# Neighbourhood attention: the low parts of the keys in a tile of their own for each head, with zeros in the other head's rows

## The chip, the core and the metric

The kernel runs on one core of one Trainium2 chip. The metric is the device time in microseconds of one execution. The core has five engines with a queue each: TensorE (PE; its weight loads are recorded as PEld), VectorE (DVE), ScalarE (ACT), GpSimd (POOL) and SyncE (SP), which issues most of the DMAs.

## The reference

Two layers of a diffusion backbone, over 512 latent tokens and 256 context tokens of 1024 features. Layer 0 has neighbourhood attention (8 heads of 64) beside a bidirectional mLSTM (4 heads of 128), layer 1 a latent attention; each layer ends in a gated feed-forward network with a depthwise convolution. The change lies in the neighbourhood attention, of which this is the core:

```python
def row_block(args):                       # one row of the 64-wide grid
    ...
    s_lat = jnp.einsum('bqhd,bkhd->bhqk', q_row, k_band).astype(jnp.float32) * scale + bias
    s_ctx = jnp.einsum('bqhd,bkhd->bhqk', q_row, k_c).astype(jnp.float32) * scale
    p = jax.nn.softmax(jnp.concatenate([s_lat, s_ctx], axis=-1), axis=-1).astype(v.dtype)
    nl = kh * GRID_W
    return (jnp.einsum('bhqk,bkhd->bqhd', p[..., :nl], v_band)
            + jnp.einsum('bhqk,bkhd->bqhd', p[..., nl:], v_c))
```

A latent query sees its window of 8 rows by 16 columns and all context keys; context queries see the context keys. All is in float32.

## The kernel before

To keep float32 accuracy with faster products, each operand is split into a high part (rounded to the type fp32r) and a low part (the rest, rounded too), and the products high x high, high x low and low x high are added up in PSUM. A linear projection is thus three products for each tile of 128 input features (`proj_steps`, one step of three products at a time).

**The heads come in pairs.** Four pairs, `p_` = 0 to 3. `na_proj` projects queries, keys and values of a pair (PSUM tiles `qp`, `kp`, `vp`) and makes for each head `s` of the pair:

- `qs[s]`, 128 rows: the high part of the head's 64 query rows in its own rows (`r0:r1`), their low part in the other head's rows;
- `kd[s]`, 128 rows: the high part of the head's keys, twice, in both halves;
- `kl`, one tile for both heads: the low part of the keys, head 0 in rows 0 to 63, head 1 in rows 64 to 127.

One product of `qs[s]` with `kd[s]` over 128 rows so gives (q high + q low) x k high. A second product, over the head's 64 rows alone, adds q high x k low.

**Scores.** `na_attn` takes 4 blocks of 128 queries for each head. A block has four products of 256 columns into one PSUM tile `sp`: high and low with the latent window, high and low with the context. Then DVE adds the bias and takes the maximum (line 816), ACT takes the exponential, DVE the reciprocal of the sum and POOL scales (tile `P`). `weighted` transposes P (`ptp`), copies it out (`pT`) and multiplies it with the values (`ops`). `scores_c` and `weighted_c` do the same for the context's own queries (`spc`, `Pc`, `ptc`, `opc`): one set of four products for each head. The score tiles take turns in three PSUM banks (`ps_w`).

**What fills the waits.** While a pair is in attention, PE gets the projections of the next pair in between (`fill`, a number of steps behind each block); for the last pair it gets the first products of the output projection (`yps`). Pair 0's first blocks run while the mLSTM's last head ends: DVE normalises its output (`mix`, in `ml_out`), and PE transposes it (`hTp`). Pairs 0 and 2 keep their tiles in the pool `nqr`, pairs 1 and 3 in `nql`; each tile is used again two pairs later. The framework that builds the program sets the order on each engine; each engine runs its queue in order.

The weights of the depthwise convolution of both layers lie in one constant tile `fcw`, loaded by a DMA of POOL's at the start and used in `up_post` of the feed-forward networks.

Of the kernel before, what the change touches and what calls it, by code (L numbers as in the profile page):

```python
# [9 lines left out]
F32 = mybir.dt.float32  # L10
# [56 lines left out]
def hybrid_backbone_kernel(ctx: ExitStack, tc: tile.TileContext, *aps):  # L67
# [14 lines left out]
    def psum_open(**n):  # L82
        """n: tiles per tag; A tiles hold two banks, the others one"""
        if psum:
            psum["st"].close()
        st = ExitStack()
        psum["st"], psum["n"], psum["split"] = st, n, False
        psum["p"] = st.enter_context(tc.tile_pool(name="ps" + "".join(f"{k}{v}" for k, v in n.items()), bufs=1,
                                                  space=bass.MemoryType.PSUM, reuse_waits="tile"))
# [41 lines left out]
    fcw = cload("ffn_conv", [128, 2, 2 * NH, 4])  # L131
# [26 lines left out]
    def table(func, after):  # L158
        """has the activation table loaded ahead of its first use"""
        t = tiny.tile([128, 8], F32, tag="rv", name="tab")  # L160
        act(t[:, 0:1], after, func)

    def fr(ap):
        return ap.bitcast(F32)
# [18 lines left out]
    def proj(o, w, x, cols, ks=tuple(range(KD)), first=True, last=True):  # L183
        """out[m, cols] = sum over k tiles of W[k, m]^T x[k, cols]; w units hold [k][128]."""
        whi, wlo = w
        xhi, xlo = x
        for lo, hi, oo in cols:
            for k in ks:
                wh = whi[:, k * 128:(k + 1) * 128]
                wl = wlo[:, k * 128:(k + 1) * 128]  # L190
                oa = o[:, oo:oo + hi - lo]
                mm(oa, wh, xhi[:, k, lo:hi], first and k == ks[0], False)
                mm(oa, wh, xlo[:, k, lo:hi], False, False)
                mm(oa, wl, xhi[:, k, lo:hi], False, last and k == ks[-1])
# [50 lines left out]
    def ada(l, part, get, pool, bufs):  # L245
        """modulation part (1024 columns) of layer l; column group j of the array takes 256 of them"""
        acc = None
        for k in range(KD):
            yield
            acc = acc or get("ada")  # L250
            w = pool.tile([128, 4, 256], F32, tag="aw", name="aw", bufs=bufs)
            nc.sync.dma_start(out=w, in_=a["ada_w"][l, part, k].rearrange("p (a b) -> p a b", a=4))
            for j in range(4):
                PE.matmul(out=acc[32 * j:32 * j + 32, 0:256], lhsT=s32[:, k, :], rhs=w[:, j, :],
                          start=k == 0, stop=k == KD - 1, tile_position=(0, 32 * j))
        row = scratch("arow")
        act(row[:, 0:256], acc[:, 0:256])
        pt = get("adat")
        for b in range(2):
            mm(pt[:, 8 * b:8 * b + 8], row[:, b * 128:(b + 1) * 128], sel[:, 0:8], True, True)  # L260
        m = mod[l][:, part * 8:(part + 1) * 8, :].rearrange("p (j b) i -> p j b i", b=2)
        tt(V, m, pt[:, 0:16].rearrange("p (b j i) -> p j b i", b=2, i=2),
           adab[:, l, part * 8:(part + 1) * 8].rearrange("p (j b) -> p j b", b=2).unsqueeze(3)
           .to_broadcast([128, 4, 2, 2]), ALU.add)

    def ada_q(l, part, q, get, pool, bufs):
        """256 columns of a part; column group j of the array takes a quarter of the k tiles"""
# [16 lines left out]
    def ada_v(l, part, hf, nv, get, pool):  # L284
        """half a part of the modulation on the vector engine: the k tiles are scaled and added up, then the
        tensor engine sums over the partitions"""
# [40 lines left out]
    def mod_scale(l, part, norm, name, nv=2):  # L327
        """norm_g * (1 + scale)"""
        t = const.tile([128, KD, nv], F32, name=name)
        ts(V, t, mod[l][:, part * 8:(part + 1) * 8, 0:nv], 1.0, None, ALU.add, ALU.bypass)  # L330
        tt(V, t, t, ng[:, l, norm, :].unsqueeze(2).to_broadcast([128, KD, nv]), ALU.mult)
        return t
# [10 lines left out]
    class Seg:  # L343
        """a run of tokens: width, offset in the padded layout, offset in the packed one, modulation column"""
# [12 lines left out]
    def rstd_bc(pss, n, dim, name):  # L357
        """PSUM [128, n*128]: rstd of every token on all partitions"""
        return bcasts(rstd_of(pss[:, :n], n, dim), n, name)
# [15 lines left out]
    def step(n):  # L375
        """n steps of the norm chains in flight, oldest first"""
        while n and chains:
            try:
                next(chains[0][1])
                n -= 1  # L380
            except StopIteration:
                chains.pop(0)

    def until(sg):
        """finish the chain of a run of tokens"""
# [3 lines left out]
    def sums4(ps, w, srcs, first, last):  # L389
        """column sums of four tiles, side by side in the array"""  # L390
# [4 lines left out]
    def sums_bc(ps, sg, name):  # L395
        """rstd on all partitions from the sums of sums4"""
# [7 lines left out]
    class YNorm:  # L404
        """sum of squares over the feature tiles of a branch output, then the gated residual"""
# [27 lines left out]
        def chain(self, x, y, Gt, mod=None, done=None):  # L433
            """x(k) += y(k) * rstd * G, then h hi/lo = split(x(k) * rstd * A + B) with mod = (A, B, h), or done(k);
            a feature tile per step, y as scratch"""
# [38 lines left out]
    # =============================== layer 0 ===============================  # L474
# [4 lines left out]
    with ExitStack() as l0:  # L479
# [38 lines left out]
        def x0_scale(q):  # L518
            """x * rstd * A for a quarter of the feature tiles"""
# [16 lines left out]
        def token_major(which, wus):  # L536
            """W[k, 512] with tokens on the output partitions; a k tile per step"""
# [39 lines left out]
        # gate rows, four feature tiles side by side in the array; the shift comes in with the bias  # L577
# [58 lines left out]
        # tri[:, 0]: k <= m ; tri[:, 1]: k >= m ; tri[:, 2]: row 127 ; tri[:, 3]: row 0  # L636
# [12 lines left out]
        # additive masks: msk[:, 0] allows column <= row, msk[:, 1] allows column >= row  # L649
# [9 lines left out]
        # running maxima of e along the scan, chunks and heads on partitions (the directions 32 apart)  # L659
# [52 lines left out]
        # -M in three exact pieces (rows 0, 32, 64 on), for its sums over the partitions to be rows of it  # L712
# [30 lines left out]
        def na_proj(p_, nq, res):  # L743
            """queries, keys and values of a pair of heads, in steps"""
# [19 lines left out]
            kl = nq.tile([128, T], F32R, tag="kl", name="kl")  # L764
            for s in range(2):
                r0, r1 = (0, 64) if s == 0 else (64, 128)
                act(kd[s][r0:r1, :], kp_[r0:r1, 0:T])
                tt(V, kl[r0:r1, :], kp_[r0:r1, 0:T], fr(kd[s][r0:r1, :]), ALU.subtract)
# [22 lines left out]
        def na_attn(p_, nw, bias_t, fill, qs, kd, kl, vtok):  # L791
# [6 lines left out]
            def scores(s):  # L798
# [8 lines left out]
                for j in range(4):  # L807
                    sp = ps_w("sp")
                    q_ = qs[s][:, j * 128:(j + 1) * 128]
                    qh_ = qs[s][r0:r1, j * 128:(j + 1) * 128]  # L810
                    lat = sp[:, 0:256].rearrange("p (f r c) -> p f r c", f=2, r=8)
                    mm(lat, q_, klat(kd[s], j), True, False)
                    mm(lat, qh_, klat(kl[r0:r1], j), False, True)
                    mm(sp[:, 256:512], q_, kd[s][:, TX:T], True, False)
                    mm(sp[:, 256:512], qh_, kl[r0:r1, TX:T], False, True)
# [30 lines left out]
            def scores_c(s):  # L846
                r0, r1 = rows[s]
                sp = ps_w("spc")
                for j in range(2):
                    q_ = qs[s][:, TX + j * 128:TX + (j + 1) * 128]  # L850
                    qh_ = qs[s][r0:r1, TX + j * 128:TX + (j + 1) * 128]
                    mm(sp[:, j * 256:(j + 1) * 256], q_, kd[s][:, TX:T], True, False)
                    mm(sp[:, j * 256:(j + 1) * 256], qh_, kl[r0:r1, TX:T], False, True)
# [47 lines left out]
        if True:  # L901
# [4 lines left out]
            def ml_in(hd):  # L906
                qk = []
                for w_ in range(2):
# [9 lines left out]
                    # 2 silu(u) = (tanh(u / 2) + 1) u  # L918
# [16 lines left out]
            def ml_decay(hd, sT):  # L935
                """decay matrices times scores, both directions"""
                ws = []
                for d in range(2):
                    pump(MP[0][d])
                    # w^T[s, t]; fwd admits s <= t  # L940
# [108 lines left out]
        with ExitStack() as nas:  # L1049
# [16 lines left out]
            def wo_steps():  # L1066
                """the first output tiles but for the last pair of heads"""
# [28 lines left out]
        mix_split(3)  # L1096
# [49 lines left out]
    def ffn(l, segs, osegs, parts, xs, h, accp, acc, Gt, groups, mod=None, done=lambda sg, k: None,  # L1146
# [5 lines left out]
        with ExitStack() as fs:  # L1152
# [3 lines left out]
            def up_post(j, pus, c0, w):  # L1156
                """depthwise conv, gate and split of one run of tokens"""
                us = []
                for g in range(2):
                    pu = pus[g]  # L1160
                    u = fw.tile([128, pw], F32, tag=f"u{g}", name=f"u{g}")[:, c0:c0 + w]
                    cw = fcw[:, l, g * NH + j, :]
# [4 lines left out]
                if j not in hid:  # L1167
                    # the last one has the place of a conv tile that is no longer needed
# [17 lines left out]
            def front(js):  # L1186
                """the first hidden tiles, a run of tokens at a time as its norm gets ready"""
# [103 lines left out]
    # =============================== layer 1 ===============================  # L1291
# [28 lines left out]
    with ExitStack() as l1a:  # L1320
# [4 lines left out]
        def rms_small(srcs, sg, gains, dim, dst):  # L1325
            """dst hi/lo[k] = split(rms_norm(src[k]) * gain[k]) for one run of tokens"""
# [72 lines left out]
    with ExitStack() as l1b:  # L1399
# [35 lines left out]
        def scores(hd):  # L1435
            """one block of queries per step"""
# [23 lines left out]
        def weighted(hd):  # L1460
            """transposes of one block of keys per step, the products a step later"""
# [45 lines left out]
        def split_mix(k):  # L1507
            """hi and lo of the outputs of a pair of heads, in the places of tiles that are no longer needed"""
# [37 lines left out]
    psum_open(A=2, w=2, c=2)  # L1546
    accp = ctx.enter_context(tc.tile_pool(name="accp1", bufs=1, reuse_waits="tile"))

    class Tiles:
        """feature tiles that lie apart"""  # L1550
# [26 lines left out]
def _prep(x, c, ctx, c_ctx, ada_w, ada_b, norm_g, ffn_w_up, ffn_conv_w, ffn_conv_b, ffn_w_down,  # L1577
# [4 lines left out]
    def feat(v):  # L1582
        """[..., n*128] -> [128, ..., n]"""
# [3 lines left out]
    def ktile(w):  # L1587
        """[nk*128, n] -> [128, nk, n]"""
        return np.asarray(w).reshape(-1, 128, w.shape[-1]).transpose(1, 0, 2)

    def mtiles(w):
        """[1024, n*128] -> [n, 128, 8*128]: unit n holds the k tiles of 128 output columns"""
# [96 lines left out]
```

## Time and profile before

| | |
|---|---|
| median of 3 runs | 1886.98 us (1885.5 to 1888.87) |
| span of the profiled execution | 1887.4 us, 26712 instructions |
| the profiled execution's own time | not recorded beside its span; the span lies 0.4 us above the median |
| mean granted TensorE clock | 0.984 |
| neighbourhood attention | about 289 to 505 us of the span |

A row of a timeline has: start and length in us, engine, line of the kernel, operation, tiles (out<-in), for a product the rows and columns of the array (128\*128), the moving operand's shape, how many instructions are merged, and in brackets the engine's idle time before it and what ended it. Products are pipelined: the length of one reaches into the next ones, so that what a product costs is read from start to start. L141 is the helper that issues every product, so a product is told by its tiles. A row of a tile's view has the count, the shortest, median and longest duration in ns, first and last start in us, and the shapes.

### The profile page before, as it was taken

Reading aid. Unit: us, or ns where it says so; the run is one execution under the profiler, and the core shown is the slowest. Engines: PE = TensorE matmul, PEld = TensorE weight load, DVE = VectorE, ACT = ScalarE, POOL = GpSimd, SP = SyncE. Lnnn points to the kernel's source line nnn. Section 1 sums busy time; section 2 is a strip of 40 time slices with the busy share of each in tenths; the row PEclk is TensorE's granted clock in tenths of the full one; section 3 lists DMA queues with packets and bytes.
Section 4 is the critical chain, followed back from the end, with each engine's and each line's share of the span. In section 5 each row is a group of like instructions: output and inputs, shape, how many; then the busy total and the mean of one; then the engine's idle time right before and its main releaser. Section 6 shows DMA issues by size and latency. Waiting matters only on the chain. (4 is left out here: it accounts for less than half of the span.)

```text
span 1887.4 us, 26712 instructions
## 1 busy us (share of the span) xinstructions
PE 1825.2 (97%) x10546; PEld 1492.1 (79%) x10546; DVE 1173.2 (62%) x2230; ACT 748.0 (40%) x1295; POOL 258.8 (14%) x312
## 2 busy tenths in 40 slices
PE   7999999999999999999999999899998999999997
PEld 4777787776678888888888887778887888888885
DVE  3383676345537676767666456888885574556655
ACT  3333454343334432222221334567784444334232
POOL 1000132122222000000000002444451100000000
PEclk8999999999999999999999999999999999999998
DMA  8343431112310333434432210100011213333221
GB/s 300 107 134 112 135 101 48 48 51 78 117 40 28 107 123 112 124 111 145 134 112 78 79 57 24 41 12 13 12 34 56 68 58 99 101 94 118 89 90 45
DMA packets 63196, 162.26 MB, mean 86 GB/s; under 512 B 6256, under 2 KB 19744, under 8 KB 63072
## 3 DMA queue, kind: packets, MB, share of 16 engines
q1 hardware_dynamic: 61616, 156.52, 26.4%
q0 software_dynamic: 1312, 3.91, 0.6%
q8 instruction: 83, 1.36, 0.3%
q14 instruction: 41, 0.34, 0.1%
q10 hardware_dynamic: 144, 0.13, 0.0%
HBM read 158.44 MB, written 2.10 MB: 85 GB/s over the span
## 5 line engine op out<-in xcount | busy, mean ns | idle before, releaser
L147 ACT ACTIVATE whi<-wraw 128x1024 fp32r<-128x1024 f32 x186 | 195.5, 1059 | 466.3 <-PE pu L141 220.0
L150 DVE TENSOR_TENSOR wlo<-wraw,whi 128x1024 fp32r<-128x1024 f32 x183 | 222.9, 1224 | 223.6 <-ACT whi L147 218.0
L141 PE MATMUL pu<-h,whi 128*128 128x258 f32 (+1 forms) x1280 | 318.6, 339 | 0.0
L141 PEld LDWEIGHTS pu<-h,whi 128*128 128x128 f32 x1280 | 219.7, 189 | 28.6 <-issue 0.8
L141 PE MATMUL pd<-hid,whi 128*128 128x512 f32 (+1 forms) x864 | 233.3, 358 | 1.5 <-DVE acc L150 1.5
L141 PE MATMUL pu<-h,wlo 128*128 128x512 f32 (+1 forms) x640 | 216.8, 339 | 0.0
L141 PEld LDWEIGHTS pd<-hid,whi 128*128 128x128 f32 x864 | 152.3, 188 | 28.4 <-DVE acc L150 3.1
L150 POOL TENSOR_TENSOR ry<-rv,mhalf 128x2 f32<-128x2 f32 (+2 forms) x26 | 23.8, 915 | 1013.9 <-DVE rv L153 1011.9
L141 PE MATMUL pd<-hid,wlo 128*128 128x512 f32 (+1 forms) x432 | 153.1, 356 | 0.0
L156 DVE SCALAR_TENSOR_TENSOR u<-pu,c_ffn_conv,u 128x769 f32<-128x769 f32 (+1 forms) x156 | 138.0, 885 | 21.6 <-ACT u L147 19.7
L150 DVE TENSOR_TENSOR acc<-pd,acc 128x512 f32<-128x512 f32 (+1 forms) x192 | 109.2, 586 | 48.6 <-PE pd L141 47.3
L141 PEld LDWEIGHTS pu<-h,wlo 128*128 128x128 f32 x640 | 121.0, 189 | 13.6
L141 PE MATMUL pu<-lb,whi 128*128 128x512 f32 x304 | 119.7, 394 | 0.0
L141 PE MATMUL pu<-hb,whi 128*128 128x512 f32 x304 | 119.0, 391 | 0.0
L141 PE MATMUL pu<-hb,wlo 128*128 128x512 f32 x304 | 118.3, 389 | 0.0
L156 DVE SCALAR_TENSOR_TENSOR av<-aw,s,av 128x512 f32<-128x512 f32 x140 | 102.4, 749 | 20.4 <-DMA aw<-in_ada_w_dram 19.9
L153 POOL TENSOR_SCALAR P<-P,rl 128x768 f32<-128x768 f32 (+1 forms) x96 | 85.6, 893 | 148.3 <-DVE nm L153 60.5
L141 PEld LDWEIGHTS pd<-hid,wlo 128*128 128x128 f32 x432 | 81.2, 189 | 11.7
L147 ACT ACTIVATE u<-pu,c_ffn_conv 128x770 f32<-128x770 f32 (+1 forms) x78 | 68.4, 877 | 39.5 <-PE pu L141 39.4
L141 PE MATMUL sp<-kr,qh 128*128 128x512 f32 (+1 forms) x256 | 72.6, 359 | 4.3 <-DVE kr L150 3.3
L141 PE MATMUL yps<-h,whi 128*128 128x512 f32 (+1 forms) x256 | 69.6, 360 | 0.0
L141 PEld LDWEIGHTS pu<-hb,whi 128*128 128x128 f32 x304 | 57.1, 188 | 13.2
(442 smaller groups left out, 3861.6 us busy)
## 6 DMA issues: line engine op xcount, KB each, us to landing
wraw<-in_ffn_up_dram SPq DMA_DIRECT2D x88, 512.0 KB, 3.6
aw<-in_ada_w_dram SPq DMA_DIRECT2D x112, 256.0 KB, 2.7
wraw<-in_ffn_down_dram SPq DMA_DIRECT2D x44, 512.0 KB, 3.6
aw<-in_ada_w_dram SPq DMA_DIRECT2D x40, 512.0 KB, 4.7
wraw<-in_w_in_dram SPq DMA_DIRECT2D x20, 512.0 KB, 3.6
wraw<-in_w_tok_dram SPq DMA_DIRECT2D x8, 512.0 KB, 4.2
wraw<-in_w_out_dram SPq DMA_DIRECT2D x8, 512.0 KB, 3.5
wraw<-in_w_o_dram SPq DMA_DIRECT2D x8, 512.0 KB, 3.5
```

The lines of the kernel that those rows point to most:

```text
L141: PE.matmul(out=o, lhsT=l, rhs=r, start=start, stop=stop)
L147: S.activation(out=o, in_=i, func=func, **kw)
L150: e.tensor_tensor(out=o, in0=x, in1=y, op=op)
L153: e.tensor_scalar(out=o, in0=x, scalar1=s1, scalar2=s2, op0=op0, op1=op1)
L156: V.scalar_tensor_tensor(out=o, in0=x, scalar=s, in1=y, op0=op0, op1=op1)
```

## The change

The tile `kl` is replaced by a pair of tiles for each pool, `kl[0]` and `kl[1]`, made once by the new function `kl_pair`. At its making POOL fills the other head's 64 rows with zeros; after that DVE writes only the head's own rows, for each pair of heads anew. The low products then take all 128 rows of `qs[s]` and of `kl[s]`: the zeros meet the low part of the queries. To make room, the constant tile `fcw` keeps the convolution weights of layer 0 alone; those of layer 1 go to a tile `fcw1` in the pool `accp1`, loaded by a DMA of POOL's when that pool opens, ahead of layer 1's output projection. (Comments and docstrings are removed too.)

```diff
-    fcw = cload("ffn_conv", [128, 2, 2 * NH, 4])
+    fcw = [cload("ffn_conv", [128, 2 * NH, 4], a["ffn_conv"][:, 0])]
...
+        klz = {}
+
+        def kl_pair(nq):
+
+            if nq not in klz:
+                klz[nq] = [nq.tile([128, T], F32R, name=f"kl{s}") for s in range(2)]
+                for s in range(2):
+                    o = slice(64, 128) if s == 0 else slice(0, 64)
+                    ts(G, klz[nq][s][o, :], zpad[o, 0, 0:1].to_broadcast([64, T]), 1.0, 0.0, ALU.mult, ALU.add)
+            return klz[nq]
...
-            kl = nq.tile([128, T], F32R, tag="kl", name="kl")
+            kl = kl_pair(nq)
...
-                tt(V, kl[r0:r1, :], kp_[r0:r1, 0:T], fr(kd[s][r0:r1, :]), ALU.subtract)
+                tt(V, kl[s][r0:r1, :], kp_[r0:r1, 0:T], fr(kd[s][r0:r1, :]), ALU.subtract)
...
-                    qh_ = qs[s][r0:r1, j * 128:(j + 1) * 128]
                     lat = sp[:, 0:256].rearrange("p (f r c) -> p f r c", f=2, r=8)
                     mm(lat, q_, klat(kd[s], j), True, False)
-                    mm(lat, qh_, klat(kl[r0:r1], j), False, True)
+                    mm(lat, q_, klat(kl[s], j), False, True)
                     mm(sp[:, 256:512], q_, kd[s][:, TX:T], True, False)
-                    mm(sp[:, 256:512], qh_, kl[r0:r1, TX:T], False, True)
+                    mm(sp[:, 256:512], q_, kl[s][:, TX:T], False, True)
...
-                    qh_ = qs[s][r0:r1, TX + j * 128:TX + (j + 1) * 128]
                     mm(sp[:, j * 256:(j + 1) * 256], q_, kd[s][:, TX:T], True, False)
-                    mm(sp[:, j * 256:(j + 1) * 256], qh_, kl[r0:r1, TX:T], False, True)
+                    mm(sp[:, j * 256:(j + 1) * 256], q_, kl[s][:, TX:T], False, True)
...
-                    cw = fcw[:, l, g * NH + j, :]
+                    cw = fcw[l][:, g * NH + j, :]
...
+    fcw.append(accp.tile([128, 2 * NH, 4], F32, name="fcw1"))
+    nc.gpsimd.dma_start(out=fcw[1], in_=a["ffn_conv"][:, 1])
```

On PE, DVE, ACT and SP the order stays as it was, row for row; only tiles have other names. This is PE's queue at the first two blocks of scores of pair 0 (`sp` are the scores, the number behind a tile's name is that of the buffer; the shape is the moving operand's as the program has it):

```order
 L141 MATMUL sp<-kd_2460,qs_2190 128x256
-L141 MATMUL sp<-kl,qs_2190 128x256
+L141 MATMUL sp<-kl_2462,qs_2190 128x256
 L141 MATMUL sp<-kd_2460,qs_2190 128x256 x2
-L141 MATMUL sp<-kl,qs_2190 128x256
+L141 MATMUL sp<-kl_2462,qs_2190 128x256
 L141 MATMUL sp<-kd_2460,qs_2190 128x256
-L141 MATMUL sp<-kl,qs_2190 128x256 x2
+L141 MATMUL sp<-kl_2462,qs_2190 128x256 x2
```

Every low product stands where it stood, and reads head 0's own tile.

POOL's queue gets rows of its own. Here are the fills of the pool `nqr`, with `kw` (the mLSTM's weighted keys) and the gating of the mLSTM's output (`mix`) behind them:

```order
 L150 TENSOR_TENSOR ry<-rv,mhalf 128x6
+L153 TENSOR_SCALAR kl_2462<-zpad 64x768
+L153 TENSOR_SCALAR kl_2463<-zpad 64x768
 L150 TENSOR_TENSOR kw<-mix,wk 128x768
 L150 TENSOR_TENSOR mix<-mix,og 128x128 x6
```

The two fills stand ahead of the first `kw`. The fills of the pool `nql` stand later on the same queue, behind the gating of the mLSTM's last head:

```order
 L150 TENSOR_TENSOR mix<-mix,og 128x128 x6
+L153 TENSOR_SCALAR kl_3042<-zpad 64x768
+L153 TENSOR_SCALAR kl_3043<-zpad 64x768
 L153 TENSOR_SCALAR P<-P,rl 128x512 x2
 L150 TENSOR_TENSOR ry<-rv,mhalf 128x6
 L153 TENSOR_SCALAR P<-P,rl 128x512 x3
```

They stand ahead of the scaling of pair 0's first probabilities `P` and of the power `ry`, on which the normalised output of the mLSTM's last head waits. A fifth new row on POOL, the DMA of `fcw1`, stands behind the last scaling of layer 1's probabilities and ahead of the low part of a weight (`wlo`) of the output projection.

## The prediction

> **What bounds the kernel now.** I read the page's shares first, then the tiles that the change touches, then the stage they lie in, product by product.
>
> ```profile
> PE 1825.2 (97%) x10546; PEld 1492.1 (79%) x10546; DVE 1173.2 (62%) x2230; ACT 748.0 (40%) x1295; POOL 258.8 (14%) x312
> ...
> L141 PE MATMUL sp<-kd,qs x64: 275/383/582, 291.1 to 471.6; 128*128 128x256 f32 x64
> ...
> L141 PE MATMUL sp<-kl,qs x64: 278/381/580, 291.4 to 472.1; 64*128 64x256 f32 x64
> ...
> L141 PE MATMUL spc<-kl,qs x16: 380/382/383, 322.0 to 491.8; 64*128 64x256 f32 x16
> ```
>
> TensorE (PE) is recorded as busy for 97% of the span; VectorE (DVE) for 62%. The change touches 80 low products (sp x64, spc x16), the only ones of 64 rows. They run from 291.1 to 491.8 us, in blocks of four: high, low, high, low. That makes 40 blocks, ten for each pair of heads. The next view cuts the stage at the four pairs (the last in two).
>
> ```profile
> 289.00:345.00 56.00, 55.93 (x293) 40.34 (x293) 29.41 (x98) 22.83 (x51) 15.03 (x23) 1.00 0.12 35
> 345.00:397.00 52.00, 51.93 (x266) 37.14 (x264) 20.59 (x51) 17.77 (x40) 8.95 (x14) 1.00 0.15 46
> 397.00:455.70 58.70, 57.08 (x294) 40.53 (x294) 32.74 (x72) 21.33 (x46) 17.45 (x29) 1.00 0.13 41
> 455.70:478.70 23.00, 23.00 (x66) 14.48 (x66) 11.74 (x40) 6.46 (x17) 8.71 (x12) 0.70 0.47 153
> 478.70:505.00 26.30, 25.23 (x129) 16.35 (x128) 16.68 (x28) 7.19 (x16) 5.39 (x6) 1.00 0.26 69
> ...
> PE vtp L144 <- ACT vt L147: 1.1, 1, 1.1
> PE ptc L144 <- POOL Pc L153: 1.1, 1, 1.1
> PE opc L141 <- DVE pTc L878: 0.5, 1, 0.5
> ```
>
> Columns: length, busy PE, PEld, DVE, ACT, POOL, granted clock, DMA share, GB/s. PE is busy all the time and waits 2.7 us in 216; DVE is busy for 40 to 63%. So what PE saves here the kernel saves, until a wait appears. "Busy" hides one thing, which only start times show:
>
> ```profile
> 298.34 0.28 PE L141 MATMUL sp<-kd,qs 128*128 128x256 f32 x1
> 298.56 0.38 PE L141 MATMUL sp<-kl,qs 64*128 64x256 f32 x1
> 298.86 0.38 PE L141 MATMUL sp<-kd,qs 128*128 128x256 f32 x1
> 299.18 0.38 PE L141 MATMUL sp<-kl,qs 64*128 64x256 f32 x1
> 299.49 0.51 PE L141 MATMUL qp<-h,whi 128*128 128x256 f32 x2
> 299.83 0.29 PE L141 MATMUL qp<-h,wlo 128*128 128x256 f32 x1
> 299.95 0.40 PE L141 MATMUL qp<-h,whi 128*128 128x256 f32 x2
> 300.19 0.28 PE L141 MATMUL qp<-h,wlo 128*128 128x256 f32 x1
> 300.31 0.40 PE L141 MATMUL qp<-h,whi 128*128 128x256 f32 x2
> ```
>
> All of these move 256 columns. Between products of 128 rows the next starts 0.12 us later (three from 299.95 to 300.31). Where the height changes, it starts 0.30 to 0.32 us later (298.56, 298.86, 299.18, 299.49). The block takes 1.15 us, and the two products behind it take 0.34 instead of 0.24.
>
> **The products.** The low tile becomes 128 rows high, with zeros where the other part of the stationary tile stands, so all four products have one height. Their count and columns stay. After the change no 64-row product is left. I price a low product at the 0.12 us of the other 128-row products. A block then costs 4 x 0.12 = 0.48 us instead of 1.15 + 0.10 = 1.25: 0.77 saved. Nothing in the rows lets a padded product be cheaper than 0.12; if it kept the 0.31 of today, the saving would be nil. I take 0.12, since kd is such a tile, of the same type, against the same stationary tile. For pairs 0, 1 and 2 this gives 7.7 us each.
>
> **Pair 0, what is late next.** Here the end of the mLSTM runs on DVE, and PE's new speed meets it.
>
> ```profile
> 296.43 0.66 DVE L816 CUSTOM_DVE_ANT_0 P<-sp,bias 128x512 f32<-128x512 f32 x1
> ...
> 299.59 0.69 DVE L816 CUSTOM_DVE_ANT_0 P<-sp,bias 128x512 f32<-128x512 f32 x1 [1.08 <-PE sp L141]
> ...
> 304.20 1.98 DVE L153 TENSOR_SCALAR mix<-mix,mv,ry 128x128 f32<-128x128 f32 x6
> ...
> 304.96 0.33 PE L144 MATMUL hTp<-c_ident,mix 128*128 128x128 f32 x1
> ```
>
> Three score tiles rotate, so the fourth block (298.34) cannot start before the first is reduced (296.43 + 0.66 = 297.1). Three blocks shorter would bring PE there at about 296.0 to 296.3: about 0.8 us of wait. Then six transposes hTp (304.96 on) need the normalised mix, which DVE makes from 304.20 on. Its chain hangs on the fourth reduction (299.59), which can move up by its 1.08 us of idle time and no more. PE, after six blocks (4.6 us less the 0.8), would be there 3.8 us earlier, the data 1.1 us: 2.2 to 2.7 us of wait. Of pair 0's 7.7 us I strike 3.0.
>
> **Pairs 1 and 2.** A period of block and fill becomes 0.48 + 0.72 = 1.2 us at its shortest (six 256-column products); DVE needs 0.69 for a reduction (299.59) and short operations, so it keeps up. I strike 0.8 us each for new waits at the turn of the pairs (between none and the 1.1 us that vtp waits today): 1.6.
>
> **Pair 3, up to 478.70.** Besides the blocks there is the clock, 0.70 here, told by these rows of 3.41 us (columns as above):
>
> ```profile
> 457.73:461.14 3.41, 3.41 (x13) 1.90 (x13) 2.07 (x6) 0.30 (x2) 0.04 (x1) 1.00 0.67 245
> 461.14:464.56 3.42, 3.42 (x12) 2.02 (x12) 1.65 (x8) 1.72 (x6) 1.47 (x3) 1.00 0.45 108
> 464.56:467.97 3.41, 3.41 (x8) 1.88 (x8) 1.37 (x4) 1.40 (x4) 1.27 (x2) 0.50 1.03 402
> ...
> 474.79:478.21 3.42, 3.42 (x9) 2.65 (x9) 2.36 (x6) 0.50 (x2) 2.38 (x3) 0.50 0.28 83
> 478.21:481.62 3.41, 3.40 (x20) 2.36 (x20) 1.24 (x2) 0.60 (x1) 0.17 (x1) 1.00 0.21 73
> ```
>
> The clock halves for four rows right after a stretch in which almost only score blocks ran (x12 products, some 1.5 us of work at 0.12 us each in 3.42 us), although PE was busy all of it. My reading: the array streamed too little between the switches. Without them it streams densely, and the halving goes. The 66 products of this piece at the full pace: 32 score products at 0.12 = 3.8; 24 yps products of 512 columns at 0.23 (kp's next start, below) = 5.6; ten others (transposes, opc) about 1.6. Together 11.0 us against 23.0: 12.0 saved, less 0.5 because eight reductions of 0.69 on DVE run nearly as long as their blocks. 11.5.
>
> ```profile
> 424.79 0.40 PE L141 MATMUL kp<-h,whi 128*128 128x512 f32 x1
> 425.02 0.40 PE L141 MATMUL kp<-h,wlo 128*128 128x512 f32 x1
> ```
>
> **Pair 3, from 478.70.** Two blocks of context scores: 1.5 us, less 0.3 because the wait of ptc for POOL (1.1 above) can grow. 1.2.
>
> **The added work.** POOL gets four zero fills of 64x768 and one more DMA.
>
> ```profile
> 307.91 1.81 POOL L153 TENSOR_SCALAR qs<-qx 64x512 fp32r<-64x512 f32 x2
> ...
> 171.07 1.48 POOL L150 TENSOR_TENSOR kw<-mix,wk 128x768 f32<-128x768 f32 x1 [150.91 <-PE ip L141]
> ...
> 300.54 1.36 POOL L153 TENSOR_SCALAR P<-P,rl 128x512 f32<-128x512 f32 x2 [4.43 <-PE sp L141]
> ...
> 461.10 0.99 POOL L1110 DMA_DIRECT2D x<-in_xin_dram  x1 [4.41 <-PE opc L141]
> ...
> 1435.98 2.88 POOL L150 TENSOR_TENSOR wlo<-wraw,whi 128x1024 fp32r<-128x1024 f32 x1 [11.53 <-ACT whi L147]
> ...
> c_ffn_conv<-in_ffn_conv_dram POOLq DMA_DIRECT2D x1, 176.0 KB, 6.3
> ...
> L147 ACT ACTIVATE u<-puf,c_ffn_conv x6: 759/765/781, 1525.0 to 1536.3; 128x512 f32<-128x512 f32 x6
> ```
>
> A fill is half as long again as qs (0.9): 1.4. The first two stand ahead of kw, behind 150 us of idle POOL. The other two stand ahead of P, where POOL idles 4.43 us and P becomes ready 1.1 us sooner; 2.8 us fit into 3.3. If that cover were gone, P and the mLSTM's last power on POOL would be late by the excess, and hTp with them. The second half of the conv table is issued where POOL idles 11.53 us (an issue is 0.99) and lands within 6.3 us, some 90 us before its first use at 1525.0. Nil for all five.
>
> **Sum.** 7.7 x 3 - 3.0 - 1.6 + 11.5 + 1.2 = 31.2 us. The span of the profiled execution is 1887.4 us, 0.4 above the median of the runs, 1886.98; I take the span as that execution's time. 1887.4 - 31.2 = 1856.2, or 1855.8 from the median: 1856. Behind 505 us everything is triggered by engines that are earlier by the same amount, so I let the gain pass through to the end.
>
> [...]
>
> **The rivals.**
> *The waits eat more.* DVE, ScalarE and POOL keep their work, and PE in each pair runs into chains as in pair 0, 3 us each, with pair 3 held by ScalarE's eight exponentials (0.72 us each):
>
> ```profile
> 473.77 0.72 ACT L147 ACTIVATE P<-P,nm 128x512 f32<-128x512 f32 x1 [4.01 <-DVE nm L153]
> ```
>
>  Against it: DVE's idle half. Gain 31.2 - 2 x 2.2 - 4 = 23, 1864. Chance 0.15.
> *The halving stays* or comes back elsewhere in the stage: 13.65 us at 0.50 cost 6.8 us. Gain 24.4, 1863. For it: the row ahead of the halving (x12) is hardly lighter than the one before that (x13). Against it: pairs 0 to 2, with the same blocks among more fill, kept 1.00. Chance 0.15.
> *No effect.* The 0.31 us belong to the change of operand, not of height: 1887. Against it: qp changes operand each time at 0.12. Chance 0.03.
> *Slower.* The low products are cheap because half the array rests, and the gap belongs to the order high-low. Then each padded product adds up to its 0.12 us: 80 x 0.12 = 9.6, 1897. It decides if low products start more than 0.31 us behind the high ones. Nothing in the rows speaks for it; chance 0.03.
> The Trainium skill (TensorEngine Tiling (Array Packing), Performance Considerations) advises row tiling for a contraction of 64 or less, up to twice as fast; by it the change gives away half of 80 x 0.12, 4.8 us. The trace shows no overlap of 64-row products here.
>
> **How the numbers follow.** The forecast, 1852 to 1860, has 0.60; its ends are no new wait in pairs 1 and 2 together with part of pair 0's back (35 us) and 4 us more waits. Gains above 35 us have 0.04. With the two middle rivals the range 1850 to 1867 holds a little over 0.85. A difference within 0.2% (3.8 us) can't be told from none; faster 0.94, same 0.03, slower 0.03.
>
> **What would show it.** Each block as four products 0.12 us apart; all score rows with 128*128; a wait of PE before hTp of about 2 us; clock 1.00 throughout pair 3, and 66 products in about 11.5 us; the fills inside POOL's idle stretches; no wait for the second table. I am wrong if low products still start 0.3 us behind, if PE's waits in the stage exceed 10 us, or if a later stage gives the gain back.

## The result, and the profile after

The changed kernel takes 1857.85 us (median of 4 runs, 1854.97 to 1860.02), the kernel before 1887.34 us beside it (4 runs, 1885.5 to 1888.87): ratio 0.9845, 95% interval 0.9831 to 0.9859, 29.5 us by the medians. The profiled execution of the changed kernel has a span of 1856.2 us, 31.2 below the 1887.4 before; its own time is 1858.19, so that the own time of an execution lies 2.0 us above its span.

First the shares of the changed kernel's page and the rows of its score tiles (count, shortest/median/longest ns, first and last start):

```profile
PE 1790.7 (96%) x10546; PEld 1478.9 (80%) x10546; DVE 1171.9 (63%) x2230; ACT 747.0 (40%) x1295; POOL 262.6 (14%) x317
...
L141 PE MATMUL sp<-kd,qs x64: 277/282/416, 291.5 to 446.5; 128*128 128x256 f32 x64
...
L141 PE MATMUL sp<-kl,qs x64: 276/283/415, 291.7 to 446.6; 128*128 128x256 f32 x64
```

The context scores (`spc`) too have 128\*128 throughout. No product of 64 rows is left among the scores, and the median of a high product fell from 383 to 282 ns, though nothing about it was changed. A block with what stands around it, from the changed kernel's timeline of TensorE:

```profile
299.58 0.28 PE L141 MATMUL qp<-h,whi 128*128 128x256 f32 x1
299.69 0.28 PE L141 MATMUL sp<-kd,qs 128*128 128x256 f32 x1
299.82 0.28 PE L141 MATMUL sp<-kl,qs 128*128 128x256 f32 x1
299.94 0.28 PE L141 MATMUL sp<-kd,qs 128*128 128x256 f32 x1
300.06 0.28 PE L141 MATMUL sp<-kl,qs 128*128 128x256 f32 x1
300.17 0.28 PE L141 MATMUL qp<-h,whi 128*128 128x256 f32 x1
```

Every start lies 0.11 to 0.13 us behind the one before. The block takes 0.48 us, and the projection behind it is no longer late.

To place the gain I cut both traces at the same products: the first score product of each pair, and two points in pair 3. First three of the five stretches of the kernel before (the other two, from 455.70 and from 478.70, stand in the prediction), then the five of the changed kernel. Columns: length, busy PE, PEld, DVE, ACT, POOL, granted clock, DMA share, GB/s.

```profile
291.12:341.30 50.18, 50.11 (x260) 36.15 (x259) 24.43 (x79) 19.94 (x47) 14.09 (x21) 1.00 0.13 38
341.30:396.63 55.33, 55.26 (x281) 39.38 (x281) 23.16 (x55) 19.54 (x43) 9.89 (x16) 1.00 0.14 43
396.63:455.70 59.07, 57.45 (x294) 40.77 (x295) 33.05 (x72) 21.70 (x46) 17.45 (x29) 1.00 0.13 41
```

```profile
291.50:339.41 47.91, 44.84 (x260) 35.17 (x259) 24.71 (x80) 19.94 (x47) 15.76 (x23) 0.96 0.12 39
339.41:387.33 47.92, 47.63 (x281) 37.14 (x281) 23.19 (x56) 19.30 (x43) 9.92 (x16) 1.00 0.16 50
387.33:438.79 51.46, 49.84 (x294) 38.54 (x295) 32.53 (x72) 21.49 (x46) 17.50 (x29) 1.00 0.15 47
438.79:450.20 11.41, 11.40 (x66) 9.23 (x66) 10.06 (x36) 6.42 (x17) 6.61 (x10) 1.00 0.77 260
450.20:475.40 25.20, 24.09 (x130) 16.06 (x129) 18.29 (x33) 7.20 (x16) 7.22 (x8) 1.00 0.31 94
```

The differences of the lengths: 2.27, 7.41, 7.61, 11.59 and 1.10 us, together 30.0. The rest of the 31.2 lies outside: -0.4 ahead of 291 us and +1.6 behind 475 us, where half-clock windows differ between two executions. In pair 0 TensorE is no longer always busy (44.84 of 47.91), and its clock is 0.96 there. What it waits for between 285 and 480 us:

```profile
PE hTp L144 <- DVE mix L153: 2.2, 1, 2.2
...
PE sp L141 <- DVE mx L826: 0.7, 1, 0.7
...
PE sp L141 <- ACT Pc L147: 0.5, 2, 0.3
```

These are new; the waits for vtp (1.1), ptc (1.1) and opc (0.5) are as long as before. And the clock halves at a place where it did not before, from the changed kernel's stretches around the wait for hTp:

```profile
302.20:305.61 3.41, 1.26 (x8) 1.05 (x8) 3.03 (x12) 2.24 (x4) 1.68 (x3) 1.00 0.00 0
305.61:309.03 3.42, 3.42 (x13) 2.97 (x12) 2.03 (x5) 1.44 (x3) 3.16 (x3) 0.50 0.33 75
309.03:312.40 3.37, 3.35 (x19) 1.99 (x18) 3.25 (x12) 2.00 (x6) 0.93 (x3) 1.00 0.29 100
```

### The profile page after: what moved, and what is told of

Its sections match the earlier page's. It is cut to its first block, busy times and chain, and to the rows that moved or that the text cites. A ratio compares the mean times of both kernels' runs of the same rounds, so it can differ in the third digit from the quotient of the medians.

```text
span 1856.2 us, 26725 instructions
## 1 busy us (share of the span) xinstructions
PE 1790.7 (96%) x10546; PEld 1478.9 (80%) x10546; DVE 1171.9 (63%) x2230; ACT 747.0 (40%) x1295; POOL 262.6 (14%) x317
## 4 chain that ended last, share of the span: by engine, by line
PE 85%; DVE 7%; POOL 2%; issue 2%; ACT 2%; DMA 1%; DVEq 0%; ACTq 0%; POOLq 0%
PE pu L141 28%; PE pd L141 13%; PE yps L141 5%; PE sp L141 4%; PE qkp L141 3%; PE puf L141 3%; PE pdl L141 3%; PE vtk L141 3%; PE qp L141 2%; PE kp L141 2%; PE pt L144 2%; PE ops L141 2%; PE vp L141 2%; PE ot L141 2%; PE ysum L392 1%
## 5 line engine op out<-in xcount | busy, mean ns | idle before, releaser
L156 DVE SCALAR_TENSOR_TENSOR u<-pu,c_ffn_conv,u 128x769 f32<-128x769 f32 x80 | 81.1, 1014 | 10.2 <-ACT u L147 9.5
L141 PEld LDWEIGHTS pu<-hb,wlo 128*128 128x128 f32 x304 | 57.1, 188 | 13.3
L1460 DVE TENSOR_REDUCE mx<-sp 128x1 f32<-128x768 f32 x64 | 60.9, 951 | 10.1 <-PE sp L141 9.6
L141 PEld LDWEIGHTS pu<-lb,whi 128*128 128x128 f32 x304 | 57.1, 188 | 12.5
```

The source lines that it names most:

```text
L141: PE.matmul(out=o, lhsT=l, rhs=r, start=start, stop=stop)
L156: V.scalar_tensor_tensor(out=o, in0=x, scalar=s, in1=y, op0=op0, op1=op1)
L1460: V.reduce_max(out=mx[:, j:j + 1], in_=sp[:, 0:T], axis=AX.X)
```

## The experiments

### One part alone: the low products back on 64 rows

The changed kernel with its own tiles, fills and second table, but low products over the head's 64 rows:

```diff
-                    mm(lat, q_, klat(kl[s], j), False, True)
+                    qh_ = qs[s][r0:r1, j * 128:(j + 1) * 128]
+                    mm(lat, qh_, klat(kl[s][r0:r1], j), False, True)
...
-                    mm(sp[:, 256:512], q_, kl[s][:, TX:T], False, True)
+                    mm(sp[:, 256:512], qh_, kl[s][r0:r1, TX:T], False, True)
```

(and the same in the context scores)

> All of the change stays (two low tiles, zero fills, second convolution table), but the low products take the head's own 64 rows again. Theory A (the gain is the missing change of height between products): the time goes back to that of before, 1885 to 1889 us; a block of four score products takes 1.15 us and 0.10 behind it again, the clock halves again in pair 3. Rival (part of the gain comes from the split tiles, whose waits are finer, or from the table's move): the time stays clearly below, under 1882 us. Rival (fills or second table cost time that the gain hid): over 1890 us.

Measured: 1889.27 us, ratio 1.0005 to the kernel before (0.9996 to 1.0014). The timeline of a block, and two stretches of pair 3:

```profile
297.96 0.28 PE L141 MATMUL sp<-kd,qs 128*128 128x256 f32 x1
298.18 0.38 PE L141 MATMUL sp<-kl,qs 64*128 64x256 f32 x1
298.49 0.39 PE L141 MATMUL sp<-kd,qs 128*128 128x256 f32 x1
298.80 0.38 PE L141 MATMUL sp<-kl,qs 64*128 64x256 f32 x1
299.11 0.39 PE L141 MATMUL qp<-h,whi 128*128 128x256 f32 x1
```

```profile
460.70:464.10 3.40, 3.40 (x13) 2.00 (x12) 1.65 (x8) 1.70 (x6) 1.45 (x3) 1.00 0.44 112
464.10:477.80 13.70, 13.70 (x30) 8.89 (x31) 6.74 (x24) 4.51 (x12) 6.12 (x8) 0.50 0.39 146
```

The 0.31 us between starts are back, and so is the halving from 464 to 478 us. By themselves the split tile, the fills and the moved table are worth nothing that can be told (the interval is 0.8 us faster to 2.6 us slower); the gain hangs on the height of the low products.

### The order within a block: high, low, low, high

The kernel before, with the second half of each block turned round. The products stay, 64 rows included; a block then has two changes of height instead of four.

```diff
-                    mm(sp[:, 256:512], q_, kd[s][:, TX:T], True, False)
-                    mm(sp[:, 256:512], qh_, kl[r0:r1, TX:T], False, True)
+                    mm(sp[:, 256:512], qh_, kl[r0:r1, TX:T], True, False)
+                    mm(sp[:, 256:512], q_, kd[s][:, TX:T], False, True)
```

(and in the context scores the second block of two)

> The kernel before, with the order high, low, low, high in each block of four score products instead of high, low, high, low: two changes of height instead of four (with the one into the fill behind), the same products. Theory A: a block goes from 1.25 to about 0.86 us (0.21 + 0.22 + 0.21 + 0.22, from the single places of the trace before where two products of a height follow a change), 0.39 x 40 = 15.6 us saved, 1872 us (1868 to 1876, the lower end if the clock stays up in pair 3). Rival B (a 64-row product takes 0.31 us by itself, whatever stands beside it): no gain, 1887. Rival C (the gap belongs to the change of operand between high and low part): about half of A's gain too, so this run does not tell A from C; the next one does.

Measured: 1869.9 us, ratio 0.9903 (0.9887 to 0.992). A block, and the first 66 products of pair 3:

```profile
298.32 0.28 PE L141 MATMUL sp<-kd,qs 128*128 128x256 f32 x1
298.53 0.38 PE L141 MATMUL sp<-kl,qs 64*128 64x256 f32 x1
298.75 0.28 PE L141 MATMUL sp<-kl,qs 64*128 64x256 f32 x1
298.96 0.39 PE L141 MATMUL sp<-kd,qs 128*128 128x256 f32 x1
299.19 0.40 PE L141 MATMUL qp<-h,whi 128*128 128x256 f32 x2
```

```profile
447.32:461.54 14.22, 14.22 (x67) 9.82 (x67) 10.56 (x37) 6.47 (x17) 6.90 (x10) 1.00 0.64 224
```

The block takes 0.87 us instead of 1.15 and 0.10 behind it. The clock stays at 1.00 in pair 3, whose first 66 products take 14.22 us, against 23.00 before and 11.41 in the changed kernel. An order alone, without a zero anywhere, brings 18.5 us. That is where the price of one change can be read: the product behind a change starts 0.21 after the last one of the old height (0.09 more than 0.12), and the product after that 0.22 later (0.10 more; 298.32, 298.53, 298.75). One change costs 0.19 us; four of them are the 0.77 per block of the prediction, two are 0.38.

### Is it the height of 64 itself? All score products on 64 rows

The kernel before, with the high products on the head's 64 rows too. This leaves out low queries times high keys.

```diff
-                    mm(lat, q_, klat(kd[s], j), True, False)
+                    mm(lat, qh_, klat(kd[s][r0:r1], j), True, False)
```

(and likewise with the context)

> The kernel before, with the high products of the scores on the head's own 64 rows too; this leaves out the low part of the queries times the high part of the keys. The alternation of high and low keys stays, all four products of a block have 64 rows, and the height changes only into the block and out of it. Theory A: 0.22 + 0.12 + 0.12 + 0.21 and 0.2 around it, about 0.87 us against 1.25, 15 us saved, 1872 us (1868 to 1876). Rival B (64-row products are slow by themselves): four times 0.31, no gain or slower, 1887 or more. Rival C (the change of operand): no gain, 1887.

Measured: 1867.86 us, ratio 0.9893 (0.9878 to 0.9908). A block:

```profile
298.83 0.38 PE L141 MATMUL sp<-kd,qs 64*128 64x256 f32 x1
299.06 0.28 PE L141 MATMUL sp<-kl,qs 64*128 64x256 f32 x1
299.18 0.28 PE L141 MATMUL sp<-kd,qs 64*128 64x256 f32 x1
299.29 0.27 PE L141 MATMUL sp<-kl,qs 64*128 64x256 f32 x1
299.50 0.51 PE L141 MATMUL qp<-h,whi 128*128 128x256 f32 x2
```

Within the block, products of 64 rows follow at 0.12 us as those of 128 rows do; the dear starts are the first and the last, where the height changes. Operands change at every product here and cost nothing. So neither the low height nor the change of operand is the cause, but the change of height. Nor are the products cheaper for being half as high. What TensorE does at such a change no row here shows.

### Pair 3 alone

The changed kernel with padded low products in pair 3 only, 64 rows in pairs 0 to 2.

```diff
-                    mm(lat, q_, klat(kl[s], j), False, True)
+                    lr = slice(0, 128) if p_ == 3 else slice(r0, r1)
+                    ql_ = qs[s][lr, j * 128:(j + 1) * 128]
+                    mm(lat, ql_, klat(kl[s][lr], j), False, True)
```

> The changed kernel with padded low products in pair 3 alone; pairs 0 to 2 take 64 rows as before. Up to 455 us all is as before, so pair 3 meets the clock's windows at the same place. Theory A (the halving from 464.6 to 478.2 came because the array streamed too little between changes of height): no halving there, 11.5 + 1.2 us saved, 1874.5 us (1872 to 1877). Rival (the halving has another cause and stays 13.65 us long): 6.8 us less saved, 1881.

Measured: 1874.27 us, ratio 0.9928 (0.9914 to 0.9943), 14.1 us below the 1888.4 of the kernel before beside it. The stretch from the first score product of pair 3:

```profile
456.84:468.30 11.46, 11.44 (x66) 9.24 (x66) 10.10 (x36) 6.42 (x17) 6.64 (x10) 1.00 0.76 261
```

The same 66 products take 11.46 us at clock 1.00, in a kernel whose products are those of before up to 456 us. Twenty low products out of eighty bring nearly half of the gain, because pair 3 had the halving too. The halving of pair 3 so goes with the four changes in a block: it is there in the profiles of the kernel before and of the first experiment, and not in those of the changed kernel, of this one and of the second and third. That the array streams too little between the changes stays a reading.

### What pair 0 lost: the wait for hTp

Pair 0 gained less than forecast. Two kernels try to cover the wait, with the changed kernel once more beside them (its profile is called the second one here). The texts below put pair 0's gain at 1.8 us; cut at the first score products it is the 2.3 us above.

> The changed kernel again, as the measure for the two kernels beside it. All theories: 1857 to 1859 us, a wait of TensorE before hTp of about 2.2 us, and the clock halved from about 305.6 to 309.0 us.

It took 1857.63 us (1856.48 to 1864.17). The halving behind the wait came again, from 302.49 us, in a stage that starts 2.0 us earlier:

```profile
299.08:302.49 3.41, 1.21 (x11) 1.00 (x9) 1.96 (x8) 1.34 (x5) 2.79 (x4) 1.00 0.26 93
302.49:305.91 3.42, 3.42 (x12) 2.68 (x13) 2.31 (x7) 2.45 (x5) 2.14 (x2) 0.50 0.07 7
```

The first kernel puts the last head's transposes behind the score blocks of both heads:

```diff
-LATE3 = 1
+LATE3 = 2
```

> The changed kernel with the mLSTM's last transposes (hTp) behind both heads' score blocks of pair 0 instead of between them; the same products, in another order. Theory (pair 0 gave 1.8 us instead of 4.7 because TensorE waits 2.15 us for the normalised mix, and because the wait makes the clock halve for the 3.4 us behind it): wait before hTp under 0.5 us, no halving between 300 and 312 us, 3 to 4 us faster than the changed kernel, 1853 to 1856. Rival 1 (the wait is what DVE owes; it only moves, to ptp or to a score bank): the sum of TensorE's waits between 285 and 345 us stays at 2.5 to 3, time within 1 us of the changed kernel. Rival 2 (the halving is not bound to the wait): halving stays or moves, gain 1 to 2 us.

Measured: 1858.2 us (1857.17 to 1858.88). Waits of TensorE from 285 to 345 us, and the stretch of pair 0:

```profile
PE hTp L144 <- DVE rl L831: 1.4, 2, 1.2
PE sp L141 <- DVE mx L826: 0.6, 1, 0.6
PE hTp L144 <- DVE mix L153: 0.3, 1, 0.3
PE sp L141 <- ACT Pc L147: 0.3, 1, 0.3
```

```profile
292.89:339.26 46.37, 43.86 (x259) 33.69 (x258) 25.73 (x80) 19.93 (x47) 14.67 (x23) 1.00 0.14 40
```

Half the theory holds: no halving, and pair 0 takes 46.37 us instead of 47.91 and (second profile) 48.05. The waits did not go, though: 2.6 us against 3.1, now split into shorter ones, as the first rival said. The 1.5 us of the profile do not show in the medians (1858.2 against 1857.63); executions of one kernel lie several us apart, and in these two profiles the stage starts at 292.89 and at 289.48 us already.

The second kernel gives pair 0 more projection steps behind each score block, and fewer later:

```diff
-            nf = NF if p_ < 3 else NF3
+            nf = (3, 2, 4, 6) if p_ == 0 else NF if p_ < 3 else NF3
```

> The changed kernel with three steps of the next pair's projections behind each score block of pair 0 instead of two, and two behind each transposed column instead of three; the number of steps stays. Theory (TensorE in pair 0 waits since its score blocks got shorter, and cover of other work helps): eight steps of 9 products stand between the score blocks in place of behind them, the waits for the score bank (0.65 us) and for hTp (2.15 us) shrink to under 1 us together, the halving at 305.6 us goes, 3 to 4 us faster, 1853 to 1856. Rival 1 (the cover is then missing behind, in the transposes of P, which wait for ScalarE's copies): time within 1 us of the changed kernel, with new waits at ptp or ops. Rival 2 (halving not bound to the wait): gain 1 to 2 us.

Measured: 1856.93 us (1856.07 to 1860.06). Its longest wait from 285 to 345 us, and pair 0:

```profile
PE hTp L144 <- DVE mix L153: 2.3, 1, 2.3
```

```profile
291.90:340.17 48.27, 44.93 (x258) 34.68 (x257) 25.66 (x79) 20.05 (x47) 15.33 (x23) 0.96 0.13 39
```

This tells little: the order that came out has the transposes behind five blocks instead of six, with 41 projection products ahead of them instead of 40, so that the cover hardly grew, and wait and halving stayed. Neither kernel beats the changed one by more than can be told.

## Why the prediction was right, point by point

**The price of a product.** Right: 0.12 us for a padded product, 0.48 for a block, 0.77 saved with the two products behind. The experiments give it a cause that the prediction only read out of one trace: each change of height costs 0.19 us, four to a block. The Trainium skill (TensorEngine Tiling (Array Packing), Key Properties) says that a change of the tiling mode drains TensorE. A price at each change fits that, 0.19 us here; the drain itself no row shows.

**Pair 0: 4.7 forecast, 2.3 measured (2.1 in the second profile).** This is the step that failed in size. The waits were right: 3.0 struck, 3.0 added. Two other things were not in the sum. The products gave less than 7.7: the start-to-start times of sp, spc and qp, without the waits, added up over the timelines, fall from 18.8 to 12.2 us (second profile), 6.6. The sum had four changes in each of ten blocks, but the first two blocks of this pair are interleaved (high, low, high, high, low, high, low, low) and have six together instead of eight: 38 x 0.19 = 7.2 us. Only 0.2 us came back behind the blocks, and a block that starts after a wait has a slow first product (from 297.56 us the next start is 0.22 us away). And the wait brought a halving of the clock, in which kp and hTp take 1.4 us more (second profile). The prediction's rival that the halving "comes back elsewhere in the stage" thus happened in small, 3.4 us long instead of 13.65, and in another place. The third experiment, with two changes left in a block, has no halving in this pair, and the pair takes no longer than the 47.91 us of the changed kernel:

```profile
292.85:340.57 47.72, 45.61 (x260) 34.20 (x259) 24.54 (x78) 19.78 (x47) 14.16 (x21) 1.00 0.12 39
```

In pair 0 the last two changes of a block so bring nothing: TensorE is idle for 2.1 us there and for 3.1 in the changed kernel, whose clock halves besides.

**The halving behind the wait.** The stretch ahead of it has TensorE busy for 1.26 us of 3.41 (1.21 in the second profile); where the longest wait is 1.2 us, with the transposes behind both heads' blocks, there is none. The Trainium skill (TensorE: Matmul & The Clock Gate, Part 1) lets the clock fall to half after an idle window of about 3.4 us. Here it fell behind less: the wait was 2.2 us long, and the window was not idle throughout.

**Pairs 1 and 2: 6.9 each forecast, 7.4 and 7.6 measured.** The 0.8 struck for new waits was too much: TensorE is idle for 0.3 of 47.92 us (0.1 before) in pair 1, and for 1.6 as before in pair 2. DVE, ScalarE and POOL kept up, so the rival "the waits eat more" falls.

**Pair 3: 11.5 and 1.2 forecast, 11.6 and 1.1 measured.** Clock 1.00, 66 products in 11.4 us. DVE is busy for 10.06 of the 11.41 us there, and has 1.35 us left before its work would set the pace.

**The added work: nil, as forecast.** The fills on POOL, from the changed kernel's timeline:

```profile
134.22 1.74 POOL L153 TENSOR_SCALAR kl<-zpad 64x768 fp32r<-64x768 f32 x2 [114.24 <-PE adav L305]
...
296.60 1.74 POOL L153 TENSOR_SCALAR kl<-zpad 64x768 fp32r<-64x768 f32 x2
...
299.86 1.36 POOL L153 TENSOR_SCALAR P<-P,rl 128x512 f32<-128x512 f32 x2 [1.52 <-DVE rv L153]
```

Two fills take 1.74 us, 0.87 each, not the 1.4 that I scaled from qs, and POOL still idles for 1.52 us behind the second two. The table `fcw1` was issued at 1393.97 us, landed within 2.2 and was first read at 1493.1.

**From the stage to the end.** 30.0 us were gained in the stage and 31.2 in the span; in the second profile, counted from the stage's first score product, 29.9 at the last context block are 30.1 at the end. The gain passes through, to within what half-clock windows in the later stages add or take. Span against span the forecast of 1856.2 is what was measured; that the median is 1857.85 and not 1856 comes from the 2.0 us between span and own time, which I had set to nil, and from executions that differ. That the gain in span is the 31.2 of the sum to the tenth is luck: pair 0 gave 2.4 us less than forecast, pairs 1 and 2 gave 1.2 more, and 1.2 came from outside the stage.

The rival "slower" and the one that blamed the operands were refuted by the third experiment: 64-row products are not cheaper than 128-row ones, and changing operands costs nothing there.

## What to carry to other kernels

A TensorE that is recorded as busy can lose more than half its time between products, as in the blocks here: read start to start, and compare with the same shape elsewhere in the trace. Products of different heights in turns cost 0.19 us at each change here, more than the product itself (0.12), so give neighbouring products one height, with zeros if need be, or at least put equal heights side by side. When a stage gets faster, look at the places where it meets another engine's chain: the new wait there costs its own length, and here a half-clock window behind it.

## What the runs showed of the hardware

In the stage of the attention the granted clock halved behind two kinds of stretches: one with TensorE busy all the time but with few products (12 in 3.42 us, 13 in 3.40, with a change of height at most of them), and one with a long wait (busy for 1.26 and 1.21 us of 3.41). It did not halve behind the first row here, of the changed kernel at the turn from pair 2 to pair 3, but it did behind the third, of the kernel before in a later stage:

```profile
435.30:438.71 3.41, 2.10 (x12) 1.32 (x13) 3.41 (x8) 2.41 (x8) 0.69 (x2) 1.00 0.00 0
438.71:442.12 3.41, 3.40 (x21) 2.52 (x22) 3.05 (x7) 0.00 (x0) 0.94 (x2) 1.00 0.70 198
...
560.12:563.54 3.42, 2.45 (x21) 2.21 (x20) 0.65 (x4) 0.17 (x1) 1.02 (x1) 1.00 0.00 0
563.54:566.95 3.41, 3.41 (x17) 3.41 (x17) 2.49 (x4) 1.08 (x3) 0.31 (x1) 0.50 0.02 5
```

So neither the busy share nor the count of products decides it. The time in which the array really streams would fit these rows (in the third, eight of the products move a single column), but no view shows that time, and the reading stays open. Not tried was whether two heads' products of 64 rows can run side by side.
